# Delta net's pool on the left of SBUF and closed early; the attention's first operands loaded and v turned during the branch before

## The chip, the cores and the metric

The kernel runs on one core of a Trainium2 chip. The metric is the device time of one execution in microseconds. A core has a matrix engine (TensorE, PE in the profile; PEld is its weight loading), VectorE (DVE), ScalarE (ACT), GpSimd (POOL) and SyncE (SP), which here only issues transfers. Each engine works through its own instructions in a fixed order. SBUF is the on-chip memory, PSUM the eight banks into which matmuls write.

## The reference

A block with four parallel branches on one input x of 1024 tokens by 1024 channels, then a feed-forward part. Cut to what matters:

```python
h = rms_norm(x, norm_mix_g)
p_s5, p_sgu, p_dn_qkv, p_dn_z, p_dn_a, p_dn_b, p_dq, p_dk, p_dv, p_gate = split(h @ w_in)
y_s5, y_sgu, y_dn = (f(..) @ w_br for the state-space, gating and delta-net branches)
y_diff = diff_attention(p_dq, p_dk, p_dv, ..) @ w_br_diff
gates = sigmoid(p_gate).reshape(Bsz, L, 4, D_MODEL)
merged = gates[0] * y_s5 + gates[1] * y_sgu + gates[2] * y_dn + gates[3] * y_diff
x = x + merged @ w_out
h = rms_norm(x, norm_ffn_g)
x = x + (silu(gate) * val of causal_dwconv(h @ w_up)) @ w_down
return rms_norm(x, norm_final_g)

def diff_attention(q, k, v, ..):     # 4 heads, two maps of 32 channels each, values of 64
    s = einsum('bqhmd,bkhmd->bhmqk', qblk * 32 ** -0.5, k) - slopes * dist   # causal
    p = softmax(s)
    o = einsum('bhqk,bkhd->bqhd', p[:, :, 0] - lam * p[:, :, 1], v)
    return rms_norm(o, norm_g) * (1.0 - lam_init)
```

## The kernel before

Activations stand as [128 channels, 1024 tokens] blocks. A product of 32-bit accuracy is made from three matmuls on split operands (`hi` and `lo` parts, `mm3_steps`); a projection of one block of 128 channels takes two PSUM tiles of 24 matmuls with 512 columns. `load_in` loads a block's weights in two pieces (`raw`, issued by SP), casts the high part on ACT and takes the low part on DVE (tags `w`) or POOL (gate weights, tags `g`).

`build` runs one stage after the other: the norm; then all branches but the attention, woven from two tasks: `delta_net` (two head pairs) and a chain of `z_in` (z projection), `s5` (state space), `diff_in` (attention projections) and `sgu` (gating); then `diff`, the attention, alone; then the rest of the gate projections, the merge, the output product, and the feed-forward part. The order on PE comes from `weave`, a planner with a clock of its own for PE: it takes the first task that is ready, and a task says with `yield LAT[..]` how long its next piece waits for other engines. If no task is ready, it runs a step of the filler, the generator `gates()`: 32 blocks of gate projections, three matmuls a step (`pg` tiles, two PSUM banks, evacuated on ACT by a tanh, `gate`). The program that results is then ordered for each engine by the framework's scheduler.

`diff_in` projects q0, k0, v0, v1, q1, k1 (a pair of heads each) and writes them to DRAM: `dqq`, `dqk` as three blocks (high, high, low for q; high, low, high for k), `dv` as one. Its tile `qf` and the gating branch's tile `gv` are in pools on the right of SBUF that open one after the other.

`diff` first needs its operands. `diff_prep(pool, b)` makes them for pair b: for each of two heads (hl) and two maps (m) one tile `stkq` and one `stkk` of 105 rows: 96 rows from `dqq` or `dqk` ([3, 32, 1024] in DRAM, L957), nine rows of positions (L958), into a staging tile `stg` (two buffers), then a cast on ACT (L959) into a tile of its own. `diff_v` loads v (`qkf<-dv`, L981), turns it by transposes on PE (`ps<-consts,qkf`) and stores high and low parts in `vhl`. `diff_scores` multiplies `stkk` and `stkq` (PE tile `p`), adds the causal mask from the small tiles `cmb` and `idb` (L914), and takes the softmax; `diff_values` turns the probabilities (`pth`, `ptl`) and multiplies them with `vhl`. After the first head `diff` calls `diff_prep` for pair 1. `diff_norm` ends a pair (`stg` again, as its square).

The delta net's pool `dn` lies on the right of SBUF with a stack of its own, which ends with the whole woven stage. The attention's pool `diff` opens after it, also on the right.

Of the kernel before, what the change touches and what calls it, by code (L numbers as in the profile page):

```python
# [11 lines left out]
F32 = mybir.dt.float32  # L12
F32R = mybir.dt.float32r
# [82 lines left out]
class Builder:  # L96
# [424 lines left out]
    def delta_net(self, pool):  # L521
        for pr in range(2):
            yield from self.dn_pair(pool, pr, self.qkv)

# [338 lines left out]
    def diff_in(self):  # L863
# [4 lines left out]
        with ExitStack() as st:  # L868
            pool = self.pool(st, "dqk", side="right")
            for w, blk in (("q", B_DQ), ("k", B_DK), ("v", B_DV), ("v", B_DV + 1), ("q", B_DQ + 1), ("k", B_DK + 1)):  # L870
                b = blk % 2
                if w == "v":
                    d = self.t(self.dp, [P, L], F32, f"dv{b}")
                    self.vdram.append(d)
                else:
                    d = self.t(self.dp, [3, P, L], F32, f"dq{w}{b}")
                    self.qkdram[w, b] = d

                f = self.t(pool, [P, L], F32, "qf", 1)
                if w != "v":  # L880
                    hi, lo = self.t(pool, [P, L], F32R, "qh", 1), self.t(pool, [P, L], F32R, "ql", 1)

                def evac(s, ps):
                    if w == "q":
                        nc.scalar.activation(f[:, s], ps, AF.Copy, scale=32.0 ** -0.5)
                    else:
                        nc.scalar.copy(f[:, s], ps)
                    if w != "v":
                        self.split(hi[:, s], lo[:, s], f[:, s], nc.scalar, nc.gpsimd)

                yield from self.project(blk, evac)
                if w == "v":
                    nc.sync.dma_start(d, f)
                else:
                    for i, x in enumerate((hi, hi, lo) if w == "q" else (hi, lo, hi)):
                        nc.sync.dma_start(d[i], x.bitcast(F32))

    def diff(self, pool):
# [17 lines left out]

        vh = self.t(pool, [P, 8, 4, 128], F32R, "vhl")
        stk = [self.diff_prep(pool, 0)]
        yield LAT["prep"]

        held = None
        for h in range(4):
            b, hl = divmod(h, 2)
            for i in range(8):
# [4 lines left out]
                if not held:  # L929
                    yield LAT["dv"]  # L930
                    for x in range(2):
                        self.diff_v(pool, vh, x)
# [9 lines left out]
            if h == 0:  # L942
                stk.append(self.diff_prep(pool, 1))
# [4 lines left out]
    def diff_prep(self, pool, b):  # L948
# [4 lines left out]
        for w in "qk":  # L953
            for hm in range(4):
# [8 lines left out]
    def diff_norm(self, pool, b, ob):  # L963
        nc = self.nc
        v = nc.vector
        y = self.t(pool, [P, L], F32, "qkf", 1)
        sq = self.t(pool, [P, L], F32, "stg", 2)
# [392 lines left out]
    def build(self):  # L1360
# [5 lines left out]
        with ExitStack() as s0:  # L1366
# [5 lines left out]
            self.filler = self.gates() if "ffn" in PARTS else iter(())  # L1372
            with ExitStack() as s1:
                self.psums(s1, "psuma", pd=2, ps=4)
                self.norm_in()
                with ExitStack() as s2:
                    dn = self.pool(s2, "dn", side="right")
                    rest = [f() for n, f in (("dn", self.z_in), ("s5", self.s5), ("diff", self.diff_in), ("sgu", self.sgu)) if n in PARTS]
                    tasks = [itertools.chain(*rest)]
                    if "dn" in PARTS:  # L1380
                        with ExitStack() as s3:
                            self.weave(self.dn_scalars(dn, self.pool(s3, "dns", side="right")), self.dn_convs(dn, 0))
                        tasks.insert(0, self.delta_net(dn))
                    self.weave(*tasks)
            with ExitStack() as s1:
                self.psums(s1, "psumb", p2=2, ps=2)
                if "diff" in PARTS:
                    self.weave(self.diff(self.pool(s1, "diff", side="right")))
            if "ffn" not in PARTS:
                return  # L1390
# [337 lines left out]
PARTS = {"dn", "s5", "sgu", "diff", "ffn"}  # L1728
# [71 lines left out]
```

## Time and profile before

| | |
|---|---|
| median of 3 runs | 1791.27 us (1788.64 to 1794.94) |
| profiled execution | 1792.62 us, span 1790.8 us, mean granted clock of TensorE 0.97 |
| PE busy | 94% of the span |
| DVE busy | 65% |
| ACT busy | 38% |
| POOL busy | 31% |
| DMA | 196.08 MB, mean 109 GB/s |

The table is from the page of one profiled execution. Its span runs from the first instruction to the last; what lies around it is 1.8 us. A timeline row has start and duration in us, engine, source line and operation, out<-in by the program's names with shapes, and in brackets how long its engine had been idle and what it had waited for. A row of windows gives each engine's busy time in a stretch, the granted clock of PE (1.00 is full speed) and the share of the DMA engines.

### The profile page before, as it was taken

What the parts mean: (1) busy time and instruction counts of PE and PEld (TensorE: products, weight loads), DVE (VectorE), ACT (ScalarE), POOL (GpSimd) and SP (SyncE); (2) the same over time, 40 slices, a digit from 0 to 9 for tenths busy, and PEclk for the clock granted to TensorE, in tenths of its full rate; (3) what the DMA queues carried; (4) which work ended last, traced back from release to release, by engine and by line L of the source; (5) the groups of instructions that cost most, each with busy time, mean ns of one, the idle gap of its engine ahead of it and who ended that gap; (6) DMA issues with size and microseconds to landing.
All of it is one profiled execution on the core that took longest, in us unless ns stands there. A gap on an engine that the chain in (4) does not pass through costs nothing.

```text
span 1790.8 us, 22150 instructions
## 1 busy us (share of the span) xinstructions
PE 1691.2 (94%) x7802; PEld 1355.8 (76%) x7802; DVE 1166.4 (65%) x2151; ACT 684.4 (38%) x1204; POOL 558.3 (31%) x441
## 2 busy tenths in 40 slices
PE   7899999999899988899999899999999999999996
PEld 5676877767777866777887687888888888788885
DVE  8984956877534534768158767787787787565442
ACT  4331322212322425656221444444444544354221
POOL 2312122444211111011216543666666663000000
PEclk9899999989999998989999999999999999999998
DMA  4112232213343323221576342222222223674341
GB/s 150 67 49 65 93 88 62 78 54 91 93 141 108 103 105 134 79 80 52 198 252 227 106 141 88 73 88 86 79 83 89 80 80 118 231 247 139 106 130 47
DMA packets 114206, 196.08 MB, mean 109 GB/s; under 512 B 33312, under 2 KB 41248, under 8 KB 113584
## 3 DMA queue, kind: packets, MB, share of 16 engines
q1 hardware_dynamic: 93504, 134.54, 23.9%
q10 hardware_dynamic: 20592, 60.14, 9.4%
q8 instruction: 61, 1.00, 0.2%
q14 instruction: 49, 0.40, 0.1%
HBM read 141.62 MB, written 52.43 MB: 108 GB/s over the span
## 4 chain that ended last, share of the span: by engine, by line
PE 60%; issue 15%; DVE 14%; DMA 7%; ACT 2%; POOL 1%; SPq 1%; POOLq 0%; ACTq 0%; DVEq 0%
PE pd L89 17%; PE qb L89 14%; PE qa L89 10%; PE pg L89 9%; PE ps L89 7%; DMA stg<-in_alibi_k_dram 2%; PE ps L93 2%; DMA stg<-in_alibi_q_dram 1%; PE p L89 1%; DVE acc L1354 1%; DVE osb L673 1%; DVE row L674 1%; DVE gld L1353 1%; DVE x L408 1%; DMA raw<-in_w_in_dram 1%
## 5 line engine op out<-in xcount | busy, mean ns | idle before, releaser
L152 POOL TENSOR_TENSOR glo<-raw,ghi 128x512 fp32r<-128x512 f32 x72 | 103.6, 1440 | 420.0 <-ACT ghi L145 400.8
L89 PE MATMUL pg<-hhi,ghi 128*128 128x512 f32 x496 | 210.3, 424 | 2.8 <-ACT gate L1326 1.6
L89 PE MATMUL pg<-hhi,glo 128*128 128x512 f32 x496 | 202.0, 407 | 0.5 <-POOL glo L152 0.5
L89 PE MATMUL pg<-hlo,ghi 128*128 128x512 f32 x496 | 201.4, 406 | 0.0
L89 PE MATMUL pd<-hhi,whi 128*128 128x512 f32 x312 | 128.3, 412 | 0.0
L145 ACT CAST ghi<-raw 128x512 fp32r<-128x512 f32 x110 | 67.9, 619 | 154.9 <-DVE cv L1594 56.5
L89 PE MATMUL pd<-hhi,wlo 128*128 128x512 f32 x312 | 123.5, 396 | 2.2 <-DVE wlo L152 2.2
L89 PE MATMUL pd<-hlo,whi 128*128 128x512 f32 x312 | 123.4, 396 | 0.0
L89 PEld LDWEIGHTS pg<-hhi,ghi 128*128 128x128 f32 x496 | 97.2, 196 | 26.2 <-issue 4.4
L89 PEld LDWEIGHTS pg<-hlo,ghi 128*128 128x128 f32 x496 | 96.3, 194 | 20.2 <-issue 1.0
L89 PEld LDWEIGHTS pg<-hhi,glo 128*128 128x128 f32 x496 | 97.4, 196 | 17.5 <-issue 1.1
L89 PE MATMUL qb<-xh,whi 128*128 128x512 f32 x264 | 103.1, 391 | 1.2 <-ACT whi L145 0.8
L89 PE MATMUL qa<-xh,ghi 128*128 128x512 f32 x264 | 102.9, 390 | 1.1 <-DVE qa L1552 1.1
L89 PE MATMUL qa<-xh,glo 128*128 128x512 f32 x264 | 102.9, 390 | 0.0
L89 PE MATMUL qa<-xl,ghi 128*128 128x512 f32 x264 | 102.8, 389 | 0.0
L89 PE MATMUL qb<-xl,whi 128*128 128x512 f32 x264 | 102.8, 389 | 0.0
L89 PE MATMUL qb<-xh,wlo 128*128 128x512 f32 x264 | 102.8, 389 | 0.0
L1672 POOL TENSOR_TENSOR x<-x,rs 128x512 f32<-128x512 f32 x6 | 7.6, 1290 | 270.5 <-DMA fr<-in_w_down_dram 207.1
L145 ACT CAST whi<-raw 128x512 fp32r<-128x512 f32 x86 | 53.4, 621 | 66.9 <-PE pd L89 37.2
L1326 ACT ACTIVATE gate<-pg 128x512 f32<-128x512 f32 x62 | 36.9, 595 | 99.2 <-PE pg L89 71.4
L89 PEld LDWEIGHTS pd<-hhi,whi 128*128 128x128 f32 x312 | 59.3, 190 | 18.1 <-issue 4.7
L152 POOL TENSOR_TENSOR wlo<-fs,whi 128x512 fp32r<-128x512 f32 x42 | 59.0, 1405 | 42.4 <-ACT whi L145 42.4
(686 smaller groups left out, 4466.5 us busy)
## 6 DMA issues: line engine op xcount, KB each, us to landing
raw<-in_w_in_dram SPq DMA_DIRECT2D x104, 256.0 KB
gates<-gate ACTq DMA_DIRECT2D x32, 512.0 KB
gld<-gates ACTq DMA_DIRECT2D x32, 512.0 KB
fr<-in_w_up_dram SPq DMA_DIRECT2D x44, 256.0 KB
raw<-in_w_up_dram SPq DMA_DIRECT2D x44, 256.0 KB
gd<-cv ACTq DMA_DIRECT2D x22, 512.0 KB
fr<-in_w_dn_dram SPq DMA_DIRECT2D x22, 256.0 KB
fr<-gd SPq DMA_DIRECT2D x22, 256.0 KB
```

What stands on the lines that cost most here:

```text
L89: return self.nc.tensor.matmul(out, w, x, **kw)
L93: return self.nc.tensor.transpose(out, x, ident)
L145: eng.copy(out, in_)
L152: (e_lo or self.nc.vector).tensor_tensor(lo, src, hi.bitcast(F32), op=ALU.subtract)
L408: nc.vector.scalar_tensor_tensor(x[:, k, :], x[:, k, :], g[:, k:k + 1], self.rt[:, s], op0=ALU.mult, op1=ALU.mult)
L673: v.tensor_tensor(tv, X[:, 0:m, j].unsqueeze(2).to_broadcast(sh), Ls[:, j, j + 1:32].unsqueeze(1).to_broadcast(sh), op=ALU.mult)
L674: v.tensor_tensor(X[:, 0:m, j + 1:32], X[:, 0:m, j + 1:32], tv, op=ALU.subtract)
L1326: self.nc.scalar.activation(self.gt[i][:, s], ps, AF.Tanh, scale=0.5)
L1353: v.scalar_tensor_tensor(g[:, s], g[:, s], 1.0, ps, op0=ALU.add, op1=ALU.mult)
L1354: (v if (b + c) % 2 or b == 3 else nc.gpsimd).tensor_tensor(acc[:, c, s], acc[:, c, s], g[:, s], op=ALU.add)
L1672: g.tensor_tensor(o, o, rs, op=ALU.mult)
```

## The change

The pool `dn` opens on the left of SBUF, and `delta_net` closes it when its second pair is done. A new task part, `diff_begin`, is chained behind `delta_net`: it waits until `diff_in` has projected everything (`self.projected`), opens a pool `operands` on the left, runs `diff_prep` for pair 0 and `diff_v` for both halves of v there, in the woven stage, while the other task is in `sgu`. `diff` takes both from there, and prepares pair 1 in the same pool. `diff_prep` goes by heads: q0, q1, k0, k1, q2, q3, k2, k3 (before: all q, then all k). `diff_norm` takes its two tiles from the pool `operands`. `PARTS`, a switch that always held all parts, is gone. No computation is added or left out.

```diff
-    def delta_net(self, pool):
+    def delta_net(self, pool, stack):
         for pr in range(2):
             yield from self.dn_pair(pool, pr, self.qkv)
+        stack.close()
...
+        self.projected = True
+
+    def diff_begin(self, stack):
+
+        while not self.projected:
+            yield 1.0
+        pool = self.operands = self.pool(stack, "operands", side="left")
+        self.stk = [self.diff_prep(pool, 0)]
+        self.vhl = self.t(pool, [P, 8, 4, 128], F32R, "vhl")
+        for x in range(2):
+            yield LAT["dv"]
+            self.diff_v(pool, self.vhl, x)
...
-        vh = self.t(pool, [P, 8, 4, 128], F32R, "vhl")
-        stk = [self.diff_prep(pool, 0)]
-        yield LAT["prep"]
+        stk, vh = self.stk, self.vhl
...
-                if not held:
-                    yield LAT["dv"]
-                    for x in range(2):
-                        self.diff_v(pool, vh, x)
...
-                stk.append(self.diff_prep(pool, 1))
+                stk.append(self.diff_prep(self.operands, 1))
...
-        for w in "qk":
-            for hm in range(4):
+        for hl, w in itertools.product(range(2), "qk"):
+            for hm in range(2 * hl, 2 * hl + 2):
...
-        y = self.t(pool, [P, L], F32, "qkf", 1)
-        sq = self.t(pool, [P, L], F32, "stg", 2)
+        y = self.t(self.operands, [P, L], F32, "qkf", 1)
+        sq = self.t(self.operands, [P, L], F32, "stg", 2)
...
-                with ExitStack() as s2:
-                    dn = self.pool(s2, "dn", side="right")
-                    rest = [f() for n, f in (("dn", self.z_in), ("s5", self.s5), ("diff", self.diff_in), ("sgu", self.sgu)) if n in PARTS]
-                    tasks = [itertools.chain(*rest)]
-                    if "dn" in PARTS:
-                        with ExitStack() as s3:
-                            self.weave(self.dn_scalars(dn, self.pool(s3, "dns", side="right")), self.dn_convs(dn, 0))
-                        tasks.insert(0, self.delta_net(dn))
-                    self.weave(*tasks)
+                s2 = ExitStack()
+                dn = self.pool(s2, "dn", side="left")
+                with ExitStack() as s3:
+                    self.weave(self.dn_scalars(dn, self.pool(s3, "dns", side="right")), self.dn_convs(dn, 0))
+                self.projected = False
+                self.weave(itertools.chain(self.delta_net(dn, s2), self.diff_begin(s0)),
+                           itertools.chain(self.z_in(), self.s5(), self.diff_in(), self.sgu()))
```

In the order of instructions this shows at three places. On SP, at the end of `diff_in` and the start of the gating branch, the kernel before issues the writes of k (`dqk`), the gating branch's constants and then only weights (`raw`) up to the attention:

```order
L163 DMA raw_5206<-in_w_in_dram 128x512
L765 DMA ybr_7_68<-row_5067 128x1024
L163 DMA raw_5212<-in_w_in_dram 128x512
L896 DMA dqk_993_5024<-qh_5026 128x1024
L896 DMA dqk_993_5024<-ql_5027 128x1024
L896 DMA dqk_993_5024<-qh_5026 128x1024
L163 DMA raw_5287<-in_w_in_dram 128x512
L803 DMA ws_5119<-in_sgu_w_dram 128x512
L805 DMA tri_5121<-in_tri_dram 128x128
L808 DMA bs_5124<-in_sgu_b_dram 128x256
L163 DMA raw_5293<-in_w_in_dram 128x512
L163 DMA raw_5397<-in_w_in_dram 128x512
```

The changed kernel issues there (L964 is now the load of a stacked tile, L965 that of its nine rows, L988 that of v):

```order
L163 DMA raw_5289<-in_w_in_dram 128x512
L964 DMA stg_5151<-dqq_893_4469 96x1x1024
L965 DMA stg_5151<-in_alibi_q_dram 9x1024
L898 DMA dqk_993_5024<-qh_5026 128x1024
L898 DMA dqk_993_5024<-ql_5027 128x1024
L898 DMA dqk_993_5024<-qh_5026 128x1024
L964 DMA stg_5156<-dqq_893_4469 96x1x1024
...
L964 DMA stg_5171<-dqq_893_4469 96x1x1024
L965 DMA stg_5171<-in_alibi_q_dram 9x1024
L964 DMA stg_5176<-dqq_893_4469 96x1x1024
L965 DMA stg_5176<-in_alibi_q_dram 9x1024
L988 DMA qkf_5209<-dv_936_4700 128x1024
```

Behind the last of these come loads 7 and 8 (`stg_5181`, `stg_5186`), v1 and then the next weights, `raw_5364`, so that no weight load stands between `raw_5289` and `raw_5364`, and the two first loads of pair 1 (`stg_6056`, `stg_6061`) come right behind `raw_5370`. On ACT, at the start of the gating branch, the casts (L966) now stand among the evacuations of that branch (`gv`, L815), its sigmoids (`gt`) and the gates (L1333):

```order
L815 COPY gv_1046_5280<-pd_5293 128x512
L790 ACTIVATE gt_5319<-gv_1046_5280 128x512
L966 CAST stkk_1024_5160<-stg_5161 105x1024
L793 ACTIVATE gt_5319<-gt_5319 128x512
L966 CAST stkk_1026_5165<-stg_5166 105x1024
L815 COPY gv_1046_5280<-pd_5325 128x512
L790 ACTIVATE gt_5351<-gv_1046_5280 128x512
L1333 ACTIVATE gate_4276<-pg_4278 128x512
L1335 DMA gates_70<-gate_4276 128x1024
L966 CAST stkq_1028_5170<-stg_5171 105x1024
L793 ACTIVATE gt_5351<-gt_5351 128x512
L966 CAST stkq_1030_5175<-stg_5176 105x1024
```

Before, no cast of a stacked tile stood ahead of the gating branch's end. On PE, behind the four projection tiles (24 matmuls each, the last is `pd_5325`), there come three matmuls of the gate tile `pg_4278`, 24 of `pg_5374`, and then v's transposes:

```order
L89 MATMUL pg_5444<-hhi_80,ghi_4193 128x512
L89 MATMUL pg_5444<-hhi_80,glo_4194 128x512
L89 MATMUL pg_5444<-hlo_81,ghi_4193 128x512
L93 MATMUL ps_5211<-consts_60,qkf_5209 128x128 x4
L93 MATMUL ps_5218<-consts_60,qkf_5209 128x128 x4
```

21 more matmuls of `pg_5444` follow, and the transposes of v1 (`qkf_5251`). Between PE's last projection of `diff_in` and the first score there were 162 gate matmuls and are now 95; 23 of them stand between the gating branch's mixing products and the first score, and 18 more ahead of the first product that takes `idb`.

For pair 1, ACT's order after the change has the casts among head 1's last blocks; the load of `stkk_1211` takes the buffer that the first of them gives back:

```order
L1333 ACTIVATE gate_6515<-pg_6338 128x512
L966 CAST stkq_1207_6055<-stg_6056 105x1024
L1050 CAST pth_5938<-ps_5977 128x4x128
L1024 ACTIVATE p_1186_5959,dsum_5956<-p_1188_5965,dmx_5957 128x896
L1050 CAST pth_5940<-ps_5984 128x2x128
L1024 ACTIVATE p_1196_6019,dsum_6017<-p_1198_6021,dmx_6018 128x1024
L966 CAST stkq_1209_6060<-stg_6061 105x1024
L145 CAST ghi_6581<-raw_6583 128x512
L1062 COPY pvt_6014<-ps_6001 64x256
L966 CAST stkk_1211_6065<-stg_6066 105x1024
```

## Rows read from the trace of the kernel before

**Rows 1.** The page: busy time, share of the span, instructions

```profile
PE 1691.2 (94%) x7802; PEld 1355.8 (76%) x7802; DVE 1166.4 (65%) x2151; ACT 684.4 (38%) x1204; POOL 558.3 (31%) x441
```

**Rows 2.** Windows: length, busy time of each engine (instructions), clock, DMA share, GB/s

```profile
590.00:640.00 50.00, 50.00 (x272) 40.40 (x271) 29.28 (x68) 20.20 (x34) 5.36 (x4) 1.00 0.15 48
660.00:680.00 20.00, 11.46 (x45) 9.01 (x43) 1.29 (x2) 5.09 (x7) 0.94 (x1) 0.83 0.39 143
```

**Rows 3.** PE's timeline at the attention's start, rows with a hole ahead

```profile
659.12 0.50 PE L89 MATMUL pg<-hhi,ghi 128*128 128x512 f32 x1 [1.46 <-ACT gate L1326]
...
670.73 1.51 PE L93 MATMUL ps<-consts,qkf 128*128 128x128 f32 x6 [5.88 <-issue]
...
682.50 0.47 PE L89 MATMUL p<-stkk,stkq 105*128 105x128 f32 x1 [5.16 <-ACT stkk L959]
...
688.70 0.47 PE L89 MATMUL p<-stkk,stkq 105*128 105x128 f32 x1 [1.19 <-ACT stkk L959]
```

**Rows 4.** Windows behind the long holes, at half clock

```profile
669.00:674.00 5.00, 3.27 (x12) 3.01 (x13) 0.00 (x0) 1.54 (x2) 0.00 (x0) 0.50 0.21 84
683.00:692.00 9.00, 7.81 (x26) 6.16 (x26) 0.95 (x2) 3.43 (x8) 0.00 (x0) 0.50 0.30 105
757.00:763.00 6.00, 3.99 (x12) 3.31 (x13) 2.77 (x6) 4.09 (x7) 0.61 (x1) 0.51 0.21 81
778.00:784.00 6.00, 6.00 (x21) 5.23 (x22) 2.72 (x16) 1.19 (x4) 1.27 (x1) 0.50 0.36 131
```

**Rows 5.** SP's queue: a weight load, k's last write, first stacked load, v0's load

```profile
578.29 0.33 SPq L163 DMA_DIRECT2D raw<-in_w_in_dram  x1
...
582.79 0.46 SPq L896 DMA_DIRECT2D dqk<-qh  x1
...
648.19 0.80 SPq L957 DMA_DIRECT2D stg<-dqq  x1
...
659.86 0.36 SPq L981 DMA_DIRECT2D qkf<-dv  x1
```

**Rows 6.** ACT's timeline: the gating branch's first copy; casts 1, 6, 7, 8

```profile
586.83 0.59 ACT L813 COPY gv<-pd 128x512 f32<-128x512 f32 x1 [5.79 <-DMA dqk<-qh]
...
657.52 1.04 ACT L959 CAST stkq<-stg 105x1024 fp32r<-105x1024 f32 x1 [7.32 <-DMA stg<-in_alibi_q_dram]
...
687.60 1.04 ACT L959 CAST stkk<-stg 105x1024 fp32r<-105x1024 f32 x1 [5.15 <-DMA stg<-in_alibi_k_dram]
...
695.22 1.05 ACT L959 CAST stkk<-stg 105x1024 fp32r<-105x1024 f32 x1 [2.00 <-DMA stg<-in_alibi_k_dram]
...
700.24 1.05 ACT L959 CAST stkk<-stg 105x1024 fp32r<-105x1024 f32 x1 [2.19 <-DMA stg<-in_alibi_k_dram]
```

**Rows 7.** PE's timeline: third projection tile's start, fourth's end, behind the mixing products

```profile
590.10 0.39 PE L89 MATMUL pd<-hhi,whi 128*128 128x512 f32 x1
...
600.98 0.39 PE L89 MATMUL pg<-hhi,ghi 128*128 128x512 f32 x1
...
638.32 0.50 PE L89 MATMUL pg<-hhi,ghi 128*128 128x512 f32 x1
```

**Rows 8.** PE's timeline around pair 1's start, rows with a hole ahead

```profile
759.01 0.48 PE L89 MATMUL p<-stkk,stkq 105*128 105x128 f32 x1 [4.66 <-ACT stkk L959]
...
771.03 0.39 PE L89 MATMUL ps<-pth,vhl 128*128 128x256 f32 x1 [2.03 <-ACT pth L1043]
...
777.21 1.32 PE L89 MATMUL ps<-consts,stg 128*128 128x2 f32 x7 [1.88 <-ACT stg L968]
```

**Rows 9.** SP's queue: the load of pair 1's first stacked k

```profile
747.42 0.73 SPq L957 DMA_DIRECT2D stg<-dqk  x1
```

**Rows 10.** ACT's timeline: its cast

```profile
757.92 1.04 ACT L959 CAST stkk<-stg 105x1024 fp32r<-105x1024 f32 x1 [6.24 <-DMA stg<-in_alibi_k_dram]
```

**Rows 11.** DVE's timeline: the attention's small cast

```profile
647.86 0.23 DVE L914 CAST idb<-consts 128x128 bf16<-128x128 f32 x1 [5.93 <-DMA ybr<-gv]
```

**Rows 12.** PE's timeline in the norm at the front

```profile
55.98 0.68 PE L89 MATMUL ps<-consts,rs1y 128*128 128x128 f32 x4 [3.22 <-DVE see L248]
```

More of the change, by code (lines that the diff above doesn't have):

```diff
@@ L893, in diff_in @@
                     nc.sync.dma_start(d, f)
-                else:
-                    for i, x in enumerate((hi, hi, lo) if w == "q" else (hi, lo, hi)):
-                        nc.sync.dma_start(d[i], x.bitcast(F32))
+                    continue
+                for i, x in enumerate((hi, hi, lo) if w == "q" else (hi, lo, hi)):
+                    nc.sync.dma_start(d[i], x.bitcast(F32))
+        self.projected = True
[8 more added lines that the diff above has]
+            self.diff_v(pool, self.vhl, x)
     def diff(self, pool):
@@ L1371, in build @@
             self.pg = self.pool(s0, "psumg", space=PSUM)
-            self.filler = self.gates() if "ffn" in PARTS else iter(())
+            self.filler = self.gates()
             with ExitStack() as s1:
@@ L1375, in build @@
                 self.norm_in()
-                with ExitStack() as s2:
-                    dn = self.pool(s2, "dn", side="right")
-                    rest = [f() for n, f in (("dn", self.z_in), ("s5", self.s5), ("diff", self.diff_in), ("sgu", self.sgu)) if n in PARTS]
-                    tasks = [itertools.chain(*rest)]
-                    if "dn" in PARTS:
-                        with ExitStack() as s3:
-                            self.weave(self.dn_scalars(dn, self.pool(s3, "dns", side="right")), self.dn_convs(dn, 0))
-                        tasks.insert(0, self.delta_net(dn))
-                    self.weave(*tasks)
+                s2 = ExitStack()
[5 more added lines that the diff above has]
+                           itertools.chain(self.z_in(), self.s5(), self.diff_in(), self.sgu()))
             with ExitStack() as s1:
                 self.psums(s1, "psumb", p2=2, ps=2)
[L1387 to L1390, printed above, removed]
+                self.weave(self.diff(self.pool(s1, "diff", side="right")))
             for _ in self.filler:
@@ L1727 @@
 LAT = {'dng': 14.76, 'tok': 2.33, 'tok2': 0.31, 'rows': 7.45, 'row': 1.76, 'decay': 0.47, 'gram': 2.75, 'gram2': 0.05, 'subst': 40.0, 'inverse': 10.0, 'solve': 2.1, 'wT': 1.2, 'state': 0.72, 'u': 1.17, 'out': 10.15, 'gelu': 0.93, 'vt': 0.8, 'mix': 0.52, 's5p': 49.2, 's5': 4.25, 's5z': 2.44, 's5v': 1.98, 's5y': 8.2, 'glu': 2.84, 'dv': 3.6, 'prep': 18.0, 'p': 1.16, 'p1': 0.14, 'p2': 1.2, 'pv': 2.4, 'sq': 6.1, 'rsqrt': 3.2}
-PARTS = {"dn", "s5", "sgu", "diff", "ffn"}
 COLS = {}
```

## The prediction

> **What bounds the kernel now.** I read the page first: TensorE (PE) is busy 94% of the span [rows 1], so only what leaves PE without work, or slows it, can change the time. Then the windows around the place that the diff touches [rows 2]. Over 590 to 640, the last branch before the attention (the spatial gating), PE is busy 50.00 of 50.00 us at clock 1.00 and the DMA engines 15%: the stage where the change puts its work has nothing for PE to lose yet, and a DMA system that is nearly free. Over 660 to 680, the attention's start, PE has 11.46 of 20 us at clock 0.83. The PE timeline names the holes [rows 3]: 1.46 us behind a gate's evacuation on ACT, 5.88 us ahead of the transposes of v (`qkf`), 5.16 and 1.19 us ahead of score products that want a stacked k operand. The two long ones are followed by a stretch at clock 0.50 [rows 4], the lower of TensorE's two levels (1.2 instead of 2.4 GHz). On SP's queue the first stacked load goes out at 648.19 [rows 5] and its cast on ACT starts at 657.52 [rows 6], 9.33 us later; the eighth cast starts at 700.24, so the casts come one per (700.24 - 657.52) / 7 = 6.10 us. The pace is that of the loads, each cast having waited for its DMA.
>
> About 0.3%, 5.4 us, is what a measurement of this kernel can tell from no change. My sums are made against the profiled execution (1792.62 us, span 1790.8), which lies 1.35 us above the median of 1791.27; I take them over to the median.
>
> **What goes away.** With operands and v ready at the attention's start, the four holes go: 1.46 + 5.88 + 5.16 + 1.19 = 13.69 us. At half clock the same matmuls take twice as long, so of the 3.27 and 7.81 us of PE work in the two half-clock stretches [rows 4] one half is loss: 5.54 us. Removed: **19.2 us**. What is late next is the small casts of the attention's own pool (`idb`), which take space that the last branch's tiles give back: now they run at 647.86 on DVE, released by the write `ybr<-gv` [rows 11], 9.5 us after PE is done with that branch's mixing products (the gate matmul behind these starts at 638.32 [rows 7]). In the new order PE has 23 + 18 = 41 gate matmuls and a few scores between those products and the first one that takes `idb`: 41 x 0.227 = 9.3 us. About even: **+1**, from 0 to 3.
>
> **What the last branch gets instead.** Nothing new is computed: eight casts of 1.04 us on ACT [rows 6], eight loads, two loads and sixteen transposes of v change their place. What they meet there:
>
> 1. *SP's queue and the three writes of k.* Load 1 and load 2 now stand around the three `dqk` writes. Load 1 goes out right behind the weight load of 578.29 [rows 5], at 578.6, and takes 9.33 us as it does now, to 588.0. The last of the three writes, now issued at 582.79, lets ACT run on at 586.83, 4.0 us later [rows 6]; behind load 1 they land at 588.0 + 4.0 = 592.0. ACT's first copy of the branch (`gv`, 0.59 us) waits for exactly these, since it takes the writes' tile. PE's third projection tile, which starts at 590.10 [rows 7], needs the bank that this copy frees: 592.0 + 0.6 - 590.1 = **2.6 us** of stall.
> 2. *ACT's queue.* Casts stand ahead of evacuations: the third and the fourth ahead of the fourth `gv` copy, and the gate's evacuation behind that. PE runs two more projection tiles of 24 matmuls; at (600.98 - 590.10) / 48 = 0.227 us each [rows 7] it is done at 603.6, and with 27 gate matmuls at 609.7. Load 2 has its place behind the writes, so casts 2, 3, 4 come at about 597, 603, 609; the gate tile behind cast 4, the copy of 0.59 and the sigmoid parts is free at 611.5: **1.8 us**.
> 3. *v behind the loads.* PE then has three matmuls (to 612.2) and the transposes of v0. SP issues that load only behind loads 5 and 6, so it goes out when cast 4 gives back the second staging buffer, and lands behind load 6: 609 + 2 x 6.1 = 621, and about 1 for itself: **9.8 us**. Eight transposes and 21 gate matmuls, part of them at half clock, take PE to 629.8; v1 stands behind loads 7 and 8, 622 + 2 x 6.1 = 633.8 or so: **4.0 us**. Now v0's load goes out at 659.86 [rows 5] between loads 3 and 4, and its transposes start at 670.73 [rows 3], 10.9 us later: more than the 6.10 us that one stacked load takes.
> 4. *Weights.* No weight load stands between loads 1 and 8 on SP, so the next gate's weights go out behind v1 and wait their turn: **2.4 us** more, at most the two loads of pair 1 that follow.
>
> Stalls 20.6 us, and the holes of 9.8 and 4.0 us bring about 8 us of PE work at half clock, as holes of 5.88 and 5.16 do now: +4. The stage costs **+24.6 us**. Lower end: v does not queue behind loads (-6.1 for v0, -4.0 for v1, -1.5 of clock): 13. Upper end: every one of six loads takes the longest distance of two casts, 695.22 - 687.60 = 7.62 us [rows 6], 1.52 more each: 33.7.
>
> On the third point the trace alone does not say whether v0 waited for the load ahead or was only slow by itself. The Trainium skill ("DMA: Bandwidth & Descriptors", section "Queues, rings and completion order", HWDGE ordering) says that on each DMA engine the descriptors of one queue are consumed in ring order, and the same page lets a copy use only as many engines as divide its slowest dimension, which for a stacked source of [3, 32, 1024] would be three. By that rule v0 waits on those three for both loads, as I take it; were the sum made without it, it would be 6 us lower. The row of 10.9 us agrees with the rule.
>
> **Pair 1.** Its stalls now: 4.66, 2.03 and 1.88 us [rows 8], 8.57 together, with (3.99 + 6.00) / 2 = 5.0 us of half clock [rows 4]: 13.6 us that go if nothing takes their place. Something does: the loads now come in the order q0, q1, k0, k1, q2, q3, k2, k3, so the first head of the pair needs four loads and not six. But on ACT the casts q0 and q1 are put between evacuations of head 1's last blocks, and only when they have run does the load of k0 find a buffer. Now such a load goes out at 747.42 [rows 9] and its cast starts at 757.92 [rows 10], 10.5 us later, while PE has some 5 us of gate work to cover it: about 5 us of stall. The same happens a second time, where the second head needs k2: 5 + 5 + 1.5, and 2 x 2.5 at half clock = 16.5. Net **+2.9**, from -5 (gate work covers one of the two) to +6.
>
> **Front.** With the pool on the other side, the parameter work of the state-space branch moves on DVE from ahead of the norm's second half to behind it. PE waits there now for `rs1y` behind that work, 3.22 us [rows 12]. It must be done later, before `qtyd`, in both. I take **-1**, from -3 to 0.
>
> **Sum:** -19.2 + 1 + 24.6 + 2.9 - 1 = +8.3 us: 1792.6 + 8.3 = 1800.9 for an execution like the profiled one, 1791.3 + 8.3 = 1799.6 for the median. I say **1799.6**.
>
> **Rivals.**
> - *Faster.* The loads are hidden under a stage that has PE busy throughout and the DMA engines at 15% [rows 2], v does not queue, and gate work covers pair 1. The Trainium skill's rule to overlap DMA with compute ("Trainium Kernel Development and Optimization", Best Practices) would have it so. From rows: stage 2.6 + 1.8 + 2.4 = 6.8, pair 1 -5, front -1, against -19.2 removed: -18.4, and with 3 us of half clock left in the stage -15: 1776, from 1773 to 1786. For it: the holes it removes are all at the attention's start, and the stage before has none. Against it: PE's order puts v's transposes where four loads are still due. Chance 0.25.
> - *The stalls only change place.* The stage costs 14 to 20 us, pair 1 nothing: -19.2 + 17 + 1 + 0 - 1 = -2: 1789, within 1786 to 1796.5. Here also belongs that the change does not load early at all, because the pool's space comes too late: then the order of before returns, and so does its time. Against that part: load 1 stands in SP's order right behind the last weights of the branch, and wants only q of pair 0, which was written long before. Chance 0.27, 0.04 of it for that part.
> - *Slower* is the forecast, 1796.5 to 1812: v behind the stacked loads, and the weights behind v. It decides when the holes that the loads make in the gating branch exceed 19.2 - 1 + 1 - 2.9 = 16 us by 5.4. Chance 0.48.
>
> **Range.** In it are the stage's ends, 13 and 33.7 (-11.6 and +9.1), pair 1's (-8, +3) and the front's (-2, +1); added as independent, about -14 and +10, so 1785 to 1810. The forecast's own range is 1796 to 1812. To leave out no more than 2 in 10 I reach into the faster case to 1780: some 0.15 lies below, 0.05 above 1812. Chances: faster by over 0.3% 0.25, within 0.27, slower 0.48.
>
> **What the changed profile should show.** Right: PE no longer full at clock 1.00 in 585 to 645; a hole of about 10 us ahead of the first `ps<-consts,qkf` transposes, which land at about 622, and one of some 4 us ahead of the second; casts of `stkq` on ACT from 588 at 6 us a piece; the hole at the attention's start gone, and no half clock there; holes of about 5 us ahead of the first scores of pair 1's two heads. Wrong: v's load landing while loads 5 and 6 are still under way (the stage below 15 us, and the time below 1796); the loads 1 to 8 at well under 6 us a piece where nothing else shares the DMA engines; or pair 1's scores with no wait for `stkk`.

## The result, and the profile after

The changed kernel takes 1803.71 us (median of 5 runs, 1799.78 to 1805.55); the kernel before, run beside it, 1790.74. The ratio is 1.0072, 95% interval 1.0048 to 1.0095: slower by 0.7%, some 13 us. The profiled execution is the median run itself, span 1801.9 us, 11.1 us more than the span of before.

PE's part on the page, of the kernel after, shows the same work in a longer span [rows 1]:

```profile
PE 1689.8 (94%) x7802; PEld 1357.3 (75%) x7802; DVE 1168.8 (65%) x2151; ACT 683.5 (38%) x1204; POOL 559.4 (31%) x441
```

PE's busy time is the same within 1.4 us, so its idle time must have grown. The windows tell where. First of the kernel before (length, busy time of PE, PEld, DVE, ACT, POOL, then clock, DMA share, GB/s):

```profile
580.00:660.00 80.00, 78.54 (x397) 63.72 (x396) 37.74 (x94) 27.87 (x48) 10.24 (x8) 1.00 0.28 97
660.00:700.00 40.00, 27.62 (x110) 21.32 (x109) 8.98 (x23) 13.31 (x27) 0.94 (x1) 0.79 0.37 133
700.00:860.00 160.00, 148.30 (x834) 116.61 (x834) 118.87 (x250) 99.23 (x220) 22.14 (x17) 0.96 0.21 75
```

And of the kernel after:

```profile
580.00:660.00 80.00, 55.48 (x225) 44.90 (x224) 21.77 (x57) 25.72 (x40) 5.08 (x4) 0.81 0.38 128
660.00:700.00 40.00, 37.34 (x217) 29.96 (x216) 23.30 (x53) 13.45 (x30) 7.29 (x5) 1.00 0.22 74
700.00:860.00 160.00, 148.06 (x863) 116.82 (x862) 123.92 (x259) 96.34 (x220) 18.32 (x13) 0.96 0.19 66
```

In 580 to 660, which was full, PE is now idle for 80 - 55.48 = 24.52 us; in 660 to 700, where the attention starts, its idle time fell from 12.38 to 2.66; behind that it stayed as it was, 11.70 and 11.94. Idle time over all three: 25.54 before, 39.12 after, +13.6 us, of which 2.5 are won back outside (the spans differ by 11.1). The hole has moved from the attention's start into the branch before it, and grown on the way. PE's timeline of the kernel after has these holes of over 1.4 us between 580 and 860:

```profile
591.30 0.50 PE L89 MATMUL pd<-hhi,whi 128*128 128x512 f32 x1 [1.93 <-ACT gv L815]
...
611.66 0.50 PE L89 MATMUL pg<-hhi,ghi 128*128 128x512 f32 x1 [1.44 <-ACT gate L1333]
...
622.95 0.45 PE L93 MATMUL ps<-consts,qkf 128*128 128x128 f32 x1 [10.32 <-issue]
...
635.57 0.47 PE L93 MATMUL ps<-consts,qkf 128*128 128x128 f32 x1 [4.84 <-DMA qkf<-dv]
...
651.41 0.80 PE L89 MATMUL pd<-hhi,whi 128*128 128x512 f32 x1 [5.98 <-ACT whi L145]
...
728.11 0.58 PE L89 MATMUL p<-stkk,stkq 105*128 105x256 f32 x1 [5.36 <-ACT p L1024]
...
767.28 0.47 PE L93 MATMUL ps<-consts,p 128*128 128x128 f32 x1 [4.48 <-DVE ob L1063]
```

SP's queue of the kernel after has the last write of k, v0's load, v1's load and the first load of the weights that PE waits for at 651.41 at these times, against [rows 5]:

```profile
581.91 0.46 SPq L898 DMA_DIRECT2D dqk<-qh  x1
...
611.27 0.36 SPq L988 DMA_DIRECT2D qkf<-dv  x1
...
624.92 0.36 SPq L988 DMA_DIRECT2D qkf<-dv  x1
...
640.05 0.33 SPq L163 DMA_DIRECT2D raw<-in_w_in_dram  x1
```

v0 takes 11.7 us from issue to its transposes, v1 10.7, and these weights 10.7 to their cast on ACT at 650.75. The weights' load did not only queue. SP had waited 3.4 us for the buffer `raw`, which POOL gives back with the low parts of the gate weights before (out at 625.38, right behind v1; cast on ACT only at 638.05, behind casts 7 and 8 and v's evacuations):

```profile
638.75 2.50 POOL L152 TENSOR_TENSOR glo<-raw,ghi 128x512 fp32r<-128x512 f32 x2 [39.17 <-ACT ghi L145]
```

ACT's timeline of the kernel after shows the branch's first copy, the cast of such weights, and the two places at pair 1, against [rows 6, 10]:

```profile
590.66 0.58 ACT L815 COPY gv<-pd 128x512 f32<-128x512 f32 x1 [2.06 <-DMA dqk<-qh]
...
650.75 1.27 ACT L145 CAST whi<-raw 128x512 fp32r<-128x512 f32 x2 [9.06 <-DMA raw<-in_w_in_dram]
...
725.78 1.04 ACT L966 CAST stkk<-stg 105x1024 fp32r<-105x1024 f32 x1 [4.91 <-DMA stg<-in_alibi_k_dram]
726.85 1.11 ACT L1024 ACTIVATE p<-p,dmx 128x1024 f32<-128x1024 f32 x1
...
765.34 1.04 ACT L966 CAST stkk<-stg 105x1024 fp32r<-105x1024 f32 x1 [6.00 <-DMA stg<-in_alibi_k_dram]
```

At pair 1 ACT stands 4.91 and 6.00 us in a cast whose load is still under way. What PE waits for runs on ACT only behind it: at the first place the softmax's exponential (L1024), at the second an evacuation (`pvt`, L1062, at 766.41) that DVE's `ob` takes.

Behind the holes of the branch PE is at half clock. Four windows that lie wholly in such stretches:

```profile
593.00:596.00 3.00, 3.00 (x8) 2.33 (x8) 0.85 (x2) 0.63 (x1) 0.00 (x0) 0.50 0.43 108
614.00:626.00 12.00, 3.05 (x12) 2.79 (x13) 1.84 (x3) 4.29 (x6) 0.00 (x0) 0.50 0.35 127
634.00:640.00 6.00, 4.43 (x21) 4.44 (x22) 1.67 (x3) 4.06 (x7) 1.25 (x2) 0.50 0.37 142
648.00:654.00 6.00, 2.58 (x6) 2.10 (x7) 2.43 (x9) 1.24 (x2) 0.00 (x0) 0.50 0.23 63
```

There a matmul of 512 columns starts every 0.43 us (593.17 to 595.73), at clock 1.00 every 0.23 us (584.67 to 588.98). The four windows hold 13.06 us of PE work, so at least 6.5 us are lost by half clock.

One window of the kernel after, inside v0's hole, where stacked loads and v0 are under way and little else:

```profile
616.00:621.00 5.00, 0.00 (x0) 0.00 (x0) 0.69 (x1) 0.52 (x1) 0.00 (x0) 0.50 0.21 84
```

The DMA engines are 21% busy, 3.4 of 16 (17% by SP's queue, 4% by ACT's, which writes a gate), and everything waits for them.

### The profile page after: what moved, and what is told of

Read it like the earlier page. It is cut to its first block, busy times and chain, and to the rows that moved or that the text cites. A ratio compares the mean times of both kernels' runs of the same rounds, so it can differ in the third digit from the quotient of the medians.

```text
span 1801.9 us, 22151 instructions
## 1 busy us (share of the span) xinstructions
PE 1689.8 (94%) x7802; PEld 1357.3 (75%) x7802; DVE 1168.8 (65%) x2151; ACT 683.5 (38%) x1204; POOL 559.4 (31%) x441
## 4 chain that ended last, share of the span: by engine, by line
PE 66%; DVE 15%; DMA 8%; issue 6%; ACT 2%; POOL 2%; SPq 0%; ACTq 0%; POOLq 0%; DVEq 0%
PE qb L89 17%; PE pd L89 14%; PE qa L89 14%; PE pg L89 11%; PE ps L89 7%; DMA stg<-in_alibi_k_dram 2%; PE ps L93 1%; DMA raw<-in_w_in_dram 1%; PE p L89 1%; DVE acc L1361 1%; DVE osb L675 1%; DVE gld L1360 1%; DMA x<-x2d 1%; DVE wlo L152 1%; DMA stg<-in_alibi_q_dram 1%
## 5 line engine op out<-in xcount | busy, mean ns | idle before, releaser
L89 PE MATMUL pg<-hhi,ghi 128*128 128x512 f32 x496 | 206.3, 416 | 1.6 <-ACT gate L1333 1.6
L152 DVE TENSOR_TENSOR wlo<-raw,whi 128x512 fp32r<-128x512 f32 x57 | 45.9, 806 | 51.4 <-ACT whi L145 50.8
L1333 ACT ACTIVATE gate<-pg 128x512 f32<-128x512 f32 x62 | 37.0, 597 | 110.3 <-PE pg L89 109.7
```

Source lines behind the costliest of these rows:

```text
L89: return self.nc.tensor.matmul(out, w, x, **kw)
L152: (e_lo or self.nc.vector).tensor_tensor(lo, src, hi.bitcast(F32), op=ALU.subtract)
L1333: self.nc.scalar.activation(self.gt[i][:, s], ps, AF.Tanh, scale=0.5)
```

## The experiments

Times within one batch are compared with the kernel before on the same chip; that is the ratio given each time (the change itself: 1.0072). The kernel before took 1790.74 to 1793.15 us in these batches, so a range given in us can be off by some 2 us. Three theories were to be told apart: that single waits cost (v's place, the tile order), that the block of slow stacked loads costs whoever stands behind it, and that the loads are slow because of their shape.

**v first** (run 1): both halves of v ahead of the stacked loads.

```diff
-        self.stk = [self.diff_prep(pool, 0)]
         self.vhl = self.t(pool, [P, 8, 4, 128], F32R, "vhl")
         for x in range(2):
             yield LAT["dv"]
             self.diff_v(pool, self.vhl, x)
+        self.stk = [self.diff_prep(pool, 0)]
```

> Both halves of v are loaded and turned ahead of the stacked loads; all else as in the change. Theory A (the eight stacked loads come at 6 us a piece and whatever stands behind them on SP's queue pays): the holes of 10.3 and 4.8 us ahead of v's transposes shrink to under 4 us together, but the weights of the second gating projection, which SP issues behind loads 6 and 8, come late instead: holes of 6 to 8 us ahead of each half of them; time 1794 to 1802 us. Rival B (v's place in the order was the cost): the two holes go with their half clock and nothing takes their place: 1785 to 1789 us.

Measured: 1795.19 us, ratio 1.0007 (0.9994 to 1.0020). PE's timeline:

```profile
594.94 0.47 PE L93 MATMUL ps<-consts,qkf 128*128 128x128 f32 x1 [3.02 <-DMA qkf<-dv]
...
622.17 0.45 PE L93 MATMUL ps<-consts,gv 128*128 128x128 f32 x1 [5.21 <-DVE gv L794]
...
633.20 0.48 PE L89 MATMUL ps<-ws,vt 128*64 128x128 f32 x2 [2.95 <-DVE vt L844]
...
641.33 0.50 PE L89 MATMUL pd<-hhi,whi 128*128 128x512 f32 x1 [1.86 <-ACT whi L145]
```

Theory A in its time, not in the waiter. Of the 15.2 us ahead of v 3.0 are left, but 5.2 + 3.0 us opened at the gating branch's own transposes and mixing products, whose evacuations share ACT with the casts (the sigmoid part that `gv` waits for ran at 620.76, behind a cast that had stood 2.71 us for its load); the weights, which I had named at 6 to 8 us for each half, cost 1.9. These four holes come to 13.0 us where the change had 24.5 in the branch, and the time is that of the kernel before.

**Thirds** (run 2): each stacked load as three transfers of 32 rows.

```diff
-                nc.sync.dma_start(g[0:96, :], self.qkdram[w, b][:, 32 * hm:32 * hm + 32, :])
+                for j in range(3):
+                    nc.sync.dma_start(g[32 * j:32 * j + 32, :], self.qkdram[w, b][j, 32 * hm:32 * hm + 32, :])
```

> Each stacked load of 96 rows is issued as three transfers of 32 rows; bytes, casts and order rules as in the change. Theory A (a stacked load is slow since its source has three blocks, and only a few of the 16 DMA engines carry it): a load takes 2 to 3 us, the eight casts come at 3 us or less, all holes in the gating branch but the first go, and the casts of pair 1 hold ACT for under 2 us: 1758 to 1772 us, faster than both kernels. Rival B (the pace is set by the size or by the DRAM side): casts still come at 5 to 6 us, time 1798 to 1806 us.

Measured: 1773.9 us, ratio 0.9897 (0.9881 to 0.9914), faster than both, 1.9 us above theory A's range. Of ACT's timeline casts 4, 7 and 8:

```profile
606.76 1.04 ACT L967 CAST stkk<-stg 105x1024 fp32r<-105x1024 f32 x1
...
618.00 1.04 ACT L967 CAST stkk<-stg 105x1024 fp32r<-105x1024 f32 x1 [3.18 <-DMA stg<-in_alibi_k_dram]
...
620.60 1.04 ACT L967 CAST stkk<-stg 105x1024 fp32r<-105x1024 f32 x1 [1.55 <-DMA stg<-in_alibi_k_dram]
```

and the one long hole of PE's timeline:

```profile
622.27 0.45 PE L93 MATMUL ps<-consts,qkf 128*128 128x128 f32 x1 [10.60 <-DMA raw<-in_w_in_dram]
```

A window in that hole, in which stacked loads 7 and 8 (issued at 613.90 and 615.81) have the DMA engines almost to themselves:

```profile
614.50:617.50 3.00, 0.00 (x0) 0.00 (x0) 0.00 (x0) 0.32 (x1) 0.00 (x0) 0.81 0.73 201
```

The last two casts are 2.60 us apart, the first ones have no DMA wait at all, pair 1's holes are gone, and the loads now keep the DMA engines 73% busy at 201 GB/s, where the change had 21% at 84: theory A on the pace. But a hole of 10.60 us ahead of v stayed, which I had not expected: v's load now stands behind all eight, and these wait for a staging buffer that an early cast gives back only when ACT's order comes to it.

**Pair 1's casts on POOL** (run 3).

```diff
-                nc.scalar.copy(s, g)
+                (nc.gpsimd.tensor_copy if b else nc.scalar.copy)(s, g)
```

> The eight casts of pair 1 run on POOL and not on ACT; pair 0 as in the change. Theory A (the two holes of 5.4 and 4.5 us at pair 1's loads come from ACT standing in a cast whose load is still under way, with the softmax and the evacuations queued behind it): both holes go, and with them the half clock behind: 1788 to 1794 us, unless the gate weights' low parts, which queue behind the casts on POOL, come late (then up to 1798). Rival B (PE waits there for the stacked operands themselves): the holes stay, 1801 to 1806 us.

Measured: 1795.77 us, ratio 1.0015 (1.0005 to 1.0024), some 10 us less than the change, though 1.8 above the range for both holes gone. The largest hole of PE's timeline in 710 to 800 is

```profile
749.33 0.50 PE L89 MATMUL p<-stkk,stkq 105*128 105x512 f32 x1 [0.96 <-ACT p L1024]
```

Both holes went with the casts, though the loads are as slow as before and the branch kept its holes (1.78, 3.18, 10.12, 4.94 and 5.94 us). PE did not wait for the stacked operands of pair 1, it waited for softmax work and evacuations that stood behind their casts on ACT.

**The old tile order** (run 4): all q, then all k.

```diff
-        for hl, w in itertools.product(range(2), "qk"):
-            for hm in range(2 * hl, 2 * hl + 2):
+        for w in "qk":
+            for hm in range(4):
```

> The stacked tiles in the old order, all q and then all k; all else as in the change. Theory A (the order matters only at pair 1, where one pattern of holes takes the place of another): the gating branch keeps its holes of 10 and 5 us, pair 1 has those of the kernel before (4.7, 2.0, 1.9) in place of 5.4 and 4.5: 1799 to 1805 us. Rival B (going by heads is what costs): 1786 to 1794 us.

Measured: 1806.09 us, ratio 1.0071 (1.0052 to 1.0090), that of the change, 1.1 us above theory A's range. PE's timeline:

```profile
620.51 0.45 PE L93 MATMUL ps<-consts,qkf 128*128 128x128 f32 x1 [9.59 <-issue]
...
633.59 0.47 PE L93 MATMUL ps<-consts,qkf 128*128 128x128 f32 x1 [4.83 <-DMA qkf<-dv]
...
759.53 0.48 PE L89 MATMUL p<-stkk,stkq 105*128 105x128 f32 x1 [6.42 <-ACT stkk L966]
```

Theory A: the order exchanges one pattern of holes at pair 1 for another, and is worth nothing by itself.

**v first and thirds** (run 5): the edits of runs 1 and 2.

> v ahead of the stacked loads, and each stacked load as three transfers of 32 rows. Theory A (in the run with thirds alone the one hole left, 10.6 us ahead of v's transposes, is v behind eight loads on SP's queue): that hole and the half clock behind it go, nothing takes their place: 1756 to 1766 us, the fastest so far. Rival B (as in the run with v first alone, other work that stands behind loads and casts takes over the hole): 1768 to 1775 us.

Measured: 1775.14 us, ratio 0.9909 (0.9893 to 0.9925), no better than thirds alone. PE's timeline:

```profile
630.71 0.80 PE L89 MATMUL pg<-hhi,ghi 128*128 128x512 f32 x1 [10.02 <-ACT ghi L145]
```

Rival B: the hole of 10.6 us ahead of v became one of 10.0 ahead of the next gate weights. Here too what comes behind the block of eight pays, whether it is v or the weights.

**The kernel before with thirds** (run 6), nothing else.

> The kernel before with nothing changed but the stacked loads, each as three transfers of 32 rows. Theory A (the attention's start waited only because a stacked load took 6 us; at 3 us it is covered by the gate matmuls that stand there): the holes of 5.9, 5.2, 1.2 and 4.7 us go or fall under 1.5 each: 1762 to 1774 us, so that early loading in itself is worth less than 8 us. Rival B (what the start lacks is the time of the first load and of v, whatever their speed): 1778 us or more.

Measured: 1776.19 us, ratio 0.9909 (0.9890 to 0.9927). PE's timeline has left, of 5.88, 5.16, 1.19 and 4.66 [rows 3, 8]:

```profile
674.82 0.47 PE L89 MATMUL p<-stkk,stkq 105*128 105x128 f32 x1 [2.26 <-ACT stkk L960]
...
684.63 0.47 PE L93 MATMUL ps<-consts,qkf 128*128 128x128 f32 x1 [4.19 <-DMA qkf<-dv]
```

Nearer to theory A, 2 us beyond its range, since v's hole stayed: with fast loads the kernel without the early start is as fast as that with an early start in one block (run 5, same batch). Most of what the attention's start lost was the loads' pace, not that they start there; runs 10 and 11 show what is left.

**The pool alone** (run 7): `dn` on the left and closed early, the attention as before.

```diff
-                with ExitStack() as s2:
-                    dn = self.pool(s2, "dn", side="right")
+                s2 = ExitStack()
+                dn = self.pool(s2, "dn", side="left")
...
         for pr in range(2):
             yield from self.dn_pair(pool, pr, self.qkv)
+        stack.close()
```

> The kernel before with the delta net's pool on the left and closed early; nothing is loaded early, and the attention's order is that of before. Theory A (the pool's side only moves the small parameter work in the norm; no cost, no gain): within 3 us of the kernel before. Rival B (the other places of the tiles cost something of themselves, in the front or the delta net): 1796 us or more.

Measured: 1794.47 us, ratio 1.0020 (1.0003 to 1.0036). Between the two theories: the pool may cost some 0.2%, at the edge of what can be told. Its trace has the holes of before and no new long one. A hole of 2.22 us ahead of a delta-net product at 173.30 in the trace of before is 3.56 here and 3.58 in the change, but 2.68 in run 4, which has the same pool; a cause stays open.

**v's loads from ACT's queue** (run 8).

```diff
-        self.nc.sync.dma_start(vf, self.vdram[b])
+        self.nc.scalar.dma_start(vf, self.vdram[b])
```

> The two loads of v are issued by ACT and not by SP; v0 goes out with the first stacked load, v1 while the second is under way. Theory A (on a DMA engine v waits for what the same queue put there before): v1 arrives 3 to 5 us after its issue, although a stacked load is under way from SP; PE waits under 2 us for v, and the time is that of the run with v first or a little less, 1788 to 1797 us. Rival B (v is slow beside a stacked load whatever queue it comes from): v1 takes 9 to 11 us from its issue, as in the change, and PE has a hole of over 3 us there.

Measured: 1796.34 us, ratio 1.0026 (1.0014 to 1.0039). The last of k's three writes, v1's load, v1's transposes and the copy that waits for the writes, of SP's, ACT's, PE's and ACT's timeline:

```profile
580.55 0.37 SPq L898 DMA_DIRECT2D dqk<-qh  x1
...
586.61 0.33 ACTq L988 DMA_DIRECT2D qkf<-dv  x1
...
594.16 0.69 PE L93 MATMUL ps<-consts,qkf 128*128 128x128 f32 x2 [6.65 <-DMA qkf<-dv]
...
597.59 0.59 ACT L815 COPY gv<-pd 128x512 f32<-128x512 f32 x1 [8.51 <-DMA dqk<-qh]
```

v1 took 7.6 us, between the two theories, and PE's hole of 6.65 us for it is what rival B said: ACT's queue did not keep it clear of the rest. A hole of 8.73 us, ahead of the next weights, stands at 637.84. But v1 overtook: issued 6.1 us after the last write on SP's queue, it arrived 3.4 us before that write was through. And the writes give a series, from the last one's issue to ACT's copy: 586.83 - 582.79 = 4.0 us with no stacked load ahead on SP's queue [rows 5, 6], 590.66 - 581.91 = 8.8 with one (the change), 597.59 - 580.55 = 17.0 with two (here). That fits a transfer that has to pass, on its own queue, behind every stacked load ahead of it. In the 17.0 there is also what v1 and a third stacked load took, issued at 586.61 and 587.62 while the write was under way; how much that is was not measured.

**Spread** (run 9): `diff_prep` as a task that yields 7 us of planned time between load and cast for each of pair 0's tiles (0 for pair 1); loads as slow as ever.

```diff
-                nc.scalar.copy(s, g)
+                yield gap
+                nc.scalar.copy(s, g)
```

> As in the change, but the eight stacked tiles of pair 0 are given out 7 us of planned time apart, so that weights, evacuations and gate matmuls stand between them in every engine's order; the loads stay as slow as they are. Theory A (the cost in the gating branch is that the eight loads and casts stand in one block, which all later transfers and evacuations must pass): the holes of the branch fall from 24.5 us to under 10 in total, 1780 to 1792 us, no slower than the kernel before. Rival B (the loads cost the same wherever they stand, since they hold the queue for 48 us): 1797 us or more.

Measured: 1788.93 us, ratio 0.9982 (0.9969 to 0.9995). PE's timeline, the largest holes:

```profile
608.59 0.33 PE L93 MATMUL ps<-consts,gv 128*128 128x128 f32 x1 [3.19 <-DVE gv L794]
...
626.26 0.79 PE L89 MATMUL pd<-hhi,whi 128*128 128x512 f32 x1 [3.98 <-ACT whi L145]
...
706.82 0.44 PE L89 MATMUL p<-stkk,stkq 105*128 105x384 f32 x1 [4.00 <-ACT p L1026]
```

Theory A in its time: with the same slow loads, but with weights and evacuations between them, the loss is gone. More small holes are left than I had said: those of over 0.6 us come to 12.7 us in the branch, not under 10. The change's cost is that slow loads stand in one block, not how many there are.

**Spread, thirds and v first** (run 10): all three edits, 3.5 us between load and cast.

> v first, stacked loads as three transfers of 32 rows each, given out 3.5 us of planned time apart. Theory A (in the run with v first and thirds the hole of 10.0 us was a gate weight behind the block of stacked loads): weights now stand between them, the hole goes: 1758 to 1768 us, the fastest. Rival B (a hole of the same size opens at the next waiter): 1771 to 1777 us.

Measured: 1766.27 us (1761.22 to 1771.35), ratio 0.9861 (0.9843 to 0.9880): theory A, the fastest of all, 1.4% below the kernel before. Spread and thirds without v first was not run, so the three edits' shares aren't told apart. PE's timeline has left:

```profile
617.95 0.33 PE L89 MATMUL ps<-ws,vt 128*64 128x128 f32 x2 [2.44 <-DVE vt L844]
...
651.41 0.80 PE L89 MATMUL pd<-hhi,whi 128*128 128x512 f32 x1 [3.69 <-ACT whi L145]
```

**The kernel before with thirds and v first** (run 11): `diff_v` ahead of `diff_prep` in `diff`.

> The kernel before with stacked loads as three transfers, and v loaded ahead of them at the attention's start. Theory A (of the holes left in the run of the kernel before with thirds, 4.2 us stood ahead of v, with half clock behind): they go, 1766 to 1773 us; if this is no slower than the run with spread loads, the early start itself is worth nothing once the loads are fast. Rival B: v delays the stacked loads by as much, 1774 to 1779 us.

Measured: 1780.01 us, ratio 0.9940 (0.9925 to 0.9956), slower than run 6. PE's timeline:

```profile
681.73 0.47 PE L89 MATMUL p<-stkk,stkq 105*128 105x128 f32 x1 [3.21 <-ACT stkk L959]
...
686.08 0.47 PE L89 MATMUL p<-stkk,stkq 105*128 105x128 f32 x1 [3.29 <-ACT stkk L959]
```

Rival B and a little more: without room ahead, what v gains the scores lose. The question put to this run has an answer too: it is 13.7 us slower than run 10 in the same batch, and run 6, the best kernel without an early start, has a ratio of 0.9909 (not below 0.9890) against 0.9861 (not above 0.9880). So once the loads are fast and given out singly, the early start is worth some 0.5%.

**Halves** (run 12): two transfers for a stacked load, each of half the columns of all three blocks; the control for run 2.

```diff
-                nc.sync.dma_start(g[0:96, :], self.qkdram[w, b][:, 32 * hm:32 * hm + 32, :])
+                for j in range(2):
+                    nc.sync.dma_start(g[0:96, 512 * j:512 * j + 512], self.qkdram[w, b][:, 32 * hm:32 * hm + 32, 512 * j:512 * j + 512])
```

> As in the change, but each stacked load is issued as two transfers that each take half of the columns of all three blocks, so each still has a source of three blocks; the control for the run with thirds. Theory A (what made the loads fast there is that a piece of one block is spread over more DMA engines): casts keep a distance of 5 to 7 us, the DMA engines' share stays at about 0.2 while a load is under way, 1800 to 1809 us. Rival B (more and smaller transfers in flight are faster whatever their shape): casts 3 to 4 us apart, 1775 to 1790 us.

Measured: 1799.84 us, ratio 1.0047 (1.0030 to 1.0064), at the edge of theory A's range. ACT's timeline, casts 3 and 4:

```profile
605.54 1.05 ACT L967 CAST stkk<-stg 105x1024 fp32r<-105x1024 f32 x1 [1.62 <-DMA stg<-in_alibi_k_dram]
...
611.03 1.05 ACT L967 CAST stkk<-stg 105x1024 fp32r<-105x1024 f32 x1 [3.91 <-DMA stg<-in_alibi_k_dram]
```

and a window in its hole ahead of v0:

```profile
618.00:623.00 5.00, 0.00 (x0) 0.00 (x0) 0.69 (x1) 0.06 (x1) 0.00 (x0) 0.50 0.26 91
```

The casts are 5.5 us apart, as with one transfer of the three blocks, and the DMA engines are 26% busy (22% by SP's queue). More transfers do not help; a source of one block does. The Trainium skill ("DMA: Bandwidth & Descriptors", section "Why a DMA increments its semaphore by 16 and not by 1") states that a copy takes the largest number of engines up to 16 that divides both sides' slowest dimension. Worked out from that, as an estimate, a source of [3, 32, 1024] takes three engines and a piece of 32 rows all 16. The DMA shares agree with it: 0.21 in the change and 0.26 here with three blocks, 0.73 in run 2 with one.

## Why the prediction was right, and where its terms were off

The forecast was slower, 1799.6 us, +8.3; measured +13.0 between medians and +11.1 between the profiled executions. The direction came out for the reason given: the slow loads make holes in the gating branch that exceed those they take away. Two terms of that stage were too low, the weights and the half clock; pair 1's came out in size by luck. Step by step:

- *What goes away.* All four holes at the attention's start are gone, as said, and `idb` came late by 0.76 us, where I had +1.
- *Stall 1, the writes of k:* 2.6 said, 1.93 measured; 592.0 said for the landing, 590.66 measured.
- *Stall 2, the gate behind cast 4:* 1.8 said, 1.44 measured.
- *Stall 3, v behind the stacked loads:* 9.8 and 4.0 said, with the transposes at about 622; 10.32 and 4.84 measured, at 622.95. That v queues behind the loads was the open point. That v ahead of the loads leaves a hole of 3.0 us (run 1), and the series of 4.0, 8.8 and 17.0 us, speak for it.
- *Stall 4, the weights:* 2.4 said, 5.98 measured. This term was mis-sized, and its path was longer than I had it. I had one step, the next gate's weights behind v1. The gate's weights made no hole themselves; but their cast came late on ACT (638.05), so their buffer was free only at 640.0, and the next projection's weights, for which PE waited, went out at 640.05. By then the two first loads of pair 1 were on the queue ahead of them, and they took 10.7 us to their cast. I had taken those two loads as a bound and not as the price.
- *Stage:* 20.6 said for the holes, 1.93 + 1.44 + 10.32 + 4.84 + 5.98 = 24.5 measured. *Half clock in it:* +4 said, at least 6.5 measured. Together at least 31.0 where I had 24.6, inside the ends of the term (13 to 33.7) but near the upper one. These two, 3.6 us of weights and 2.5 of clock, are more than the whole sum lacks; smaller gains elsewhere hide it.
- *Pair 1:* 5 + 5 + 1.5 said, 5.36 and 4.48 measured, and a last one of 1.06 at the norm. The size is right by luck, since the waiter is wrong: I had PE waiting for the first scores' stacked operands. They were not wanted yet. ACT stood in the cast, and the softmax and the evacuations of the head before stood behind it (run 3 shows it). My own sign of being wrong, pair 1's scores with no wait for `stkk`, did appear.
- *Front:* the norm's products came 1.4 us earlier (`rs1y` at 54.56 instead of 55.98 [rows 12]); of that 0.9 is left at the weight load ahead of the branch, issued at 577.41 and not 578.29 [rows 5]. I had -1. In the other profiles with the pool on the left this load goes out anywhere from 575.97 to 579.83, so this agreement shows nothing.
- *Small and not foreseen:* in the merge a hole of 1.04 us (at 1003.04 in the trace of before) is gone and one of 0.83 (at 991.84) is down to 0.48, while others grew; over 860 to 1080 PE's idle time fell from 10.18 to 9.14, a gain of 1.0. It is part of why the spans differ by 11.1 where the holes around the attention grew by 13.6.

The rival *faster* needed v not to queue and gate work to cover pair 1; neither held (its sum in the prediction also left out the +1 for `idb`). The rival that the stalls only change place wanted a stage of 14 to 20 us and nothing at pair 1; the stage's holes alone were 24.5. The Trainium skill's rule to overlap DMA with compute ("Trainium Kernel Development and Optimization", Best Practices) did not hold here by itself: the loads did run beside PE's work, but PE's order, ACT's and SP's all had to pass them, and PE's busy time in 580 to 660 fell from 78.54 to 55.48; given out singly and with fast loads (run 10) the overlap did pay. The rival that the change doesn't do what it says fell: load 1 went out at 577.84.

## What to carry to other kernels

Work that is moved under another stage is hidden only if no queue has to pass it in order: count, on the issuing queue and on the engine that casts, what stands behind each moved transfer, and give the moved pieces out singly. Before moving a slow load, look at why it is slow: a DMA share of 0.2 with everything waiting pointed here to a transfer that uses few engines, and splitting it by its outer dimension was worth more (1.0%, run 2, or 0.9% without the move, run 6) than any place for it. The move alone lost 0.7%; with split loads, single pieces and v first it gave 1.4%, some 0.5% more than split loads without the move.

## What the hardware showed that was not expected

The cost of a transfer with three blocks is not its own 5 to 6 us alone, but that of all that follows on its queue: the last of three writes of 512 KB took 4.0, 8.8 and 17.0 us, from its issue to the copy that waits for it, behind none, one and two of them (the 17.0 with v1 beside it). And splitting by columns into two transfers left the pace at 5.5 us and the DMA engines 26% busy, while splitting by blocks into three brought two casts to 2.6 us apart and the engines to 73%.
